# A two-layer transformer kernel on one core: host-side feature-major inputs, NSA scores from split queries and keys, and a later start of the modulation stream

## The chip, the core and the metric

The kernel runs on one core of one Trainium2 chip. The metric is the device time of one execution in microseconds (us). Engines are named as the profile names them: PE is TensorE's matrix multiplication, PEld its weight load, DVE is VectorE, ACT is ScalarE, POOL is GpSimd, SP is SyncE.

## The reference, cut to what matters

There are S = 256 tokens of D = 2048 features, all in float32. The first block is an NSA attention mixer followed by a gated feed-forward layer; the second has its norms, shifts and gates modulated by a vector `c`, and holds an attention layer and an MLP.

```python
h    = rmsnorm(x) * mix_norm_g
proj = h @ nsa_w_in               # queries (16 heads of 128), three keys/values, gates
# per head: the scores q.k for the compressed keys (15), the selected and the window
# branch; softmax of each, gated, and o = sum over branches of p @ v
x = x + concat(o) @ nsa_w_out
x = x + ffn(rmsnorm(x))           # ffn_w_in, ffn_w_out: the largest weights of block 1

mod = silu(c) @ w_mod + b_mod     # c has 2048 entries, w_mod is 2048 x 12288
sh1, sc1, g1, sh2, sc2, g2 = split(mod, 6)
h = rmsnorm(x) * (1 + sc1) + sh1
x = x + g1 * attention(h)         # w_in, w_uq, w_ukv, w_out
h = rmsnorm(x) * (1 + sc2) + sh2
x = x + g2 * (relu(h @ w_ff1) ** 2 @ w_ff2)
out = rmsnorm(x) * final_norm_g
```

## The kernel before, in words

Every large product is made from three reduced-precision products. A float32 operand is split by `split` (L84 on ACT writes the high part, L85 on DVE the rest), and `mm3` issues three matmuls, high by high, high by low and low by high, from L127, L128 and L129. The residual `h` and the normalised inputs `x` lie feature-major: features on the 128 partitions, the 256 tokens along the row.

`gemm` streams the weights. One tile holds 2 x 128 features by 512 columns (1 MB at most): a DMA of SP's queue fills `raw` (5 buffers), ACT makes `whi` and DVE makes `wlo` (4 buffers each, 128x1024), and PE runs 24 matmuls of 256 columns with them. After every tile `step()` advances two generators: `inner`, small work of the current layer, and `fill`, a background stream. `fill` is advanced `rate` steps for each 64th of a unit of work.

The background stream is `modulation`. For each of ten segments of 1024 columns (two more run in the last MLP) `mod_columns` loads 16 tiles `mw` of 128x1024 (L736, POOL's queue, two buffers; 192 loads in all), and DVE adds each times a column of `csil` into `macc` (L740, L742). `after(ld)` ties each load to the last matmul that had been issued, so that the loads follow PE's progress. At a segment's end eight small matmuls (L723) sum `macc` over the partitions, four copies (L726) gather the sums and L727 stores them to `modv`. The stream begins before the gemm of the fourth group of keys, inside `nsa()`, with rate 4.2, and runs through the NSA scores and the feed-forward layer.

At the start `norm_x` loads `x` token-major into eight tiles `xt`, transposes them on PE (32 transposes, L341), and from the banks ACT and DVE make the split, scaled `x` (L345, L346) while DVE copies `h` (L348). ACT squares `xt` with an accumulated sum (L354); the rows' `rstd` comes from these sums. The first gemm of `nsa_w_in` uses the `x` pairs one after another, as they come.

Vectors (`mix_norm_g`, `vec1`, `pos`, the pieces of `b_mod`) are loaded as rows and turned into columns by a transpose on PE (L228).

In `nsa_head` the scores of a head are float32 matmuls of `qT` with `kT`: one of 271 columns (L588), one of 15 (L589), two of 256 (L608). A float32 matmul shows as two passes in the trace (x2 beside the row).

The order of the instructions on each engine is not written by hand. The framework's scheduler decides it from its own model of times, so that a change in one place can move rows elsewhere. `nsa()`, `norm_x()` and the rest are called by `run` at L1015 and following.

Of the kernel before, what the change touches and what calls it, by code (L numbers as in the profile page):

```python
# [66 lines left out]
class Kernel:  # L67
# [209 lines left out]
    def vectors(self):  # L277
        nc, a, m = self.nc, self.a, self.main
        vec1 = self.columns([(self.vec("ffn_norm_g", 16), 16), (self.vec("final_norm_g", 16), 16),
                             (self.vec("attn_norm_g_2", 16), 16), (self.vec("mlp_norm_g_2", 16), 16),  # L280
                             (self.vec("mla_q_norm_g_2", 3), 3), (self.vec("mla_kv_norm_g_2", 1), 1),
                             (self.vec("c_2", 16), 16)], "vec1")
# [41 lines left out]
    def norm_x(self):  # L324

        nc, a = self.nc, self.a
        self.gmix = self.columns([(self.vec("mix_norm_g", 16), 16)], "gmix", nc.sync)
        xs = [self.pair("x") for _ in range(KT)]
        xt = []
        for s in range(8):  # L330
            xt.append(self.main.tile([128, 2, S], F32, name="xt", tag="u", bufs=16))
# [3 lines left out]
        banks = (("O", 1), ("PT", 1), ("S", 2), ("S", 2))  # L335
        for s in range(8):
            p = self.bank(*banks[s % 4])
            k = 2 * s
            for i in range(2):
                for t in range(2):  # L340
                    nc.tensor.transpose(p[:, i * S + t * 128:i * S + (t + 1) * 128],  # L341
                                        xt[s][:, t, i * 128:(i + 1) * 128], self.ident)
            for i in range(2):
                g, pi = self.gmix[:, k + i:k + i + 1], p[:, i * S:(i + 1) * S]
                nc.scalar.activation(xs[k + i][:, 0, :], pi, AF.Copy, scale=g)  # L345
                nc.vector.scalar_tensor_tensor(xs[k + i][:, 1, :], pi, g, xs[k + i][:, 0, :].bitcast(F32),  # L346
                                               op0=OP.mult, op1=OP.subtract)
            nc.vector.tensor_copy(self.h[:, k:k + 2, :].rearrange("p k n -> p (k n)"), p)  # L348
        ssq = self.main.tile([128, 2, 8], F32, name="ssq")

        def squares():
            for s in range(8):
                for t in range(2):
                    nc.scalar.activation(self.slast[:, t * S:(t + 1) * S], xt[s][:, t, :], AF.Square,  # L354
                                         accum_out=ssq[:, t, s:s + 1])
                yield
        self.inner = squares()
        return xs, ssq

    def rstd_x(self, ssq):  # L360
        for _ in self.inner:
            pass
        rc = self.main.tile([128, 2], F32, name="rc_x")
        self.nc.vector.tensor_reduce(rc, ssq, AX.X, OP.add)
        self.nc.vector.tensor_scalar(rc, rc, 1.0 / D, EPS, op0=OP.mult, op1=OP.add)
        return self.rsqrt(rc, self.main, "rcx")
# [29 lines left out]
    def nsa(self, xs, ssq, mp):  # L396
        nc, a, tc = self.nc, self.a, self.tc
        W, LD = a["nsa_w_in"], 5168
        with ExitStack() as es:
# [4 lines left out]
            kT = p.tile([128, 4, 528], F32, name="kT")  # L404
# [7 lines left out]
            with tc.tile_pool(name="cmp", bufs=1) as cp:  # L412
                dtab = self.bias_table("rel_bias", 0, cp)
                pos = self.columns([(a["cmp_pos_k"].rearrange("a b c -> (a b) c"), 32),
                                    (a["cmp_pos_v"].rearrange("a b c -> (a b) c"), 32)], "pos")
# [19 lines left out]
                def evk(br):  # L435
                    def f(i, b):
                        for j in range(2):
                            kg = kT[:, 2 * i + j, :].rearrange("p (t n) -> p t n", n=264)
                            kg = bass.AP(tensor=kg.tensor, offset=kg.offset + 128 * br,
                                         ap=[list(kg.ap[0]), [272, 2], [1, 128]])  # L440
                            nc.vector.tensor_tensor(kg, b[:, j * S:(j + 1) * S].rearrange("p (t n) -> p t n", n=128),
                                                    r1.rearrange("p (t n) -> p t n", n=128), OP.mult)
# [9 lines left out]
                self.fill, self.rate = self.modulation(mp, range(10)), 4.2  # L452
# [30 lines left out]
            for g in range(4):  # L483
# [4 lines left out]
                def evq(i, b):  # L488
                    qT[i] = w.tile([128, 2, S], F32, name="qT", tag="qT", bufs=2)
                    nc.vector.tensor_tensor(qT[i], b.rearrange("p (a n) -> p a n", n=S),  # L490
                                            rq[:, None, :].to_broadcast([128, 2, S]), OP.mult)
                self.gemm(W, LD, 0, xs, [(512 * g, 512)], evq)
                for j in range(4):
                    os_.append(self.nsa_head(w, 4 * g + j, g, qT[j // 2][:, j % 2, :], bt[:, j, :],
# [28 lines left out]
    def compress(self, cp, ku, kT, vcc):  # L523
# [35 lines left out]
        nc.vector.tensor_copy(kT[:, :, 256:271], po[:, :60].rearrange("p (g c) -> p g c", c=NCMP))  # L559
# [19 lines left out]
    def nsa_head(self, w, hd, g, q, bt, kT, vt, vcc, gate):  # L579
# [4 lines left out]
        pt = w.tile([128, 10, 128], F32, name="pt", tag="pt", bufs=2)  # L584
# [607 lines left out]
```

## Time and profile before

| | us |
|---|---|
| median of the runs (3) | 2123.52 (2122.17 to 2125.51) |
| profiled execution, its own time | 2119.85 |
| its span | 2118.0 |
| PE busy | 2094.1 (99%) |
| DVE busy | 1452.0 (69%) |
| ACT busy | 1017.1 (48%) |

The span runs from the first instruction to the last in the profile of one execution; that execution's own time is 1.85 us longer, and the median lies 3.67 us above that time. Busy is the time in which an engine had at least one instruction under way. The core's granted TensorE clock was at its full level in every fortieth of the span but for the first microseconds. The stretches are the start (0 to 36 us: loads, first gemm), NSA (to about 340 us), its output product and the feed-forward layer (to about 1110 us), the second block's attention and the MLP.

### The profile page before, as it was taken

The numbers are of one execution on the slowest core, as the hardware profiler recorded it, in microseconds if no ns is written. First come the engines' busy times: TensorE is split into PE (matmuls) and PEld (weight loads), VectorE is DVE, ScalarE is ACT, GpSimd is POOL, SyncE is SP. The second block draws the span as 40 slices with busy tenths as digits, with TensorE's granted clock in tenths as the row PEclk, the third lists the DMA queues.
The fourth block names the chain that finished last, engine by engine and source line by source line (L and its number), as shares of the span: only waits on it lengthen the run. The fifth ranks groups of instructions, "written<-read, shape, count | busy, mean of one in ns | idle before, by whom it ended". The sixth has DMA issues, their size and how long they took to land. (4 is left out here: it accounts for less than half of the span.)

```text
span 2118.0 us, 40943 instructions
## 1 busy us (share of the span) xinstructions
PE 2094.1 (99%) x16405; PEld 1992.5 (94%) x16405; DVE 1452.0 (69%) x2144; ACT 1017.1 (48%) x1504; POOL 162.9 (8%) x297
## 2 busy tenths in 40 slices
PE   9999999999999999999999999999999999999998
PEld 8899999999999999999999999899889989989987
DVE  7467876787777777877867676677676555555556
ACT  6334655554434434443445465565434534534543
POOL 2211000010110111101000000000100000000000
PEclk9999999999999999999999999999999999999999
DMA  8778555889889888888975663568887656656663
GB/s 277 261 234 311 170 163 180 286 265 296 276 282 303 274 301 281 279 294 276 298 233 156 182 183 112 160 196 280 283 294 233 194 191 194 193 193 193 192 194 133
DMA packets 288302, 492.29 MB, mean 232 GB/s; under 512 B 27111, under 2 KB 139338, under 8 KB 287856
## 3 DMA queue, kind: packets, MB, share of 16 engines
q1 hardware_dynamic: 254128, 371.20, 55.2%
q0 software_dynamic: 33408, 117.70, 16.7%
q8 instruction: 128, 2.10, 0.4%
q10 hardware_dynamic: 576, 0.79, 0.1%
q14 instruction: 62, 0.51, 0.1%
HBM read 487.21 MB, written 2.20 MB: 231 GB/s over the span
## 5 line engine op out<-in xcount | busy, mean ns | idle before, releaser
L84 ACT ACTIVATE whi<-raw 128x1024 fp32r<-128x1024 f32 (+2 forms) x716 | 746.2, 1044 | 904.8 <-PE acc L128 645.4
L85 DVE TENSOR_TENSOR wlo<-raw,whi 128x1024 fp32r<-128x1024 f32 (+2 forms) x716 | 853.5, 1200 | 392.1 <-ACT whi L84 378.8
L127 PE MATMUL acc<-x,whi 128*128 128x256 f32 x3184 | 882.6, 278 | 3.2 <-ACT v L463 1.4
L128 PE MATMUL acc<-x,whi 128*128 128x256 f32 x3184 | 884.3, 278 | 0.0
L129 PE MATMUL acc<-x,wlo 128*128 128x256 f32 x3184 | 882.7, 278 | 0.2 <-DVE wlo L85 0.2
L127 PEld LDWEIGHTS acc<-x,whi 128*128 128x128 f32 x3184 | 597.8, 188 | 8.6 <-issue 5.0
L128 PEld LDWEIGHTS acc<-x,whi 128*128 128x128 f32 x3184 | 599.4, 188 | 5.4 <-issue 4.6
L129 PEld LDWEIGHTS acc<-x,wlo 128*128 128x128 f32 x3184 | 599.0, 188 | 1.4 <-DVE wlo L85 0.6
L742 DVE SCALAR_TENSOR_TENSOR macc<-mw,csil,macc 128x1024 f32<-128x1024 f32 x180 | 231.1, 1284 | 175.0 <-DMA mw<-w_mod 174.1
L128 PE MATMUL acc<-u,whi 128*128 128x256 f32 x1260 | 349.7, 279 | 0.8 <-DVE u L85 0.8
L127 PE MATMUL acc<-u,whi 128*128 128x256 f32 x1260 | 346.3, 280 | 1.0 <-DVE h L642 0.6
L129 PE MATMUL acc<-u,wlo 128*128 128x256 f32 x1260 | 347.0, 278 | 0.0
L128 PEld LDWEIGHTS acc<-u,whi 128*128 128x128 f32 x1260 | 236.7, 188 | 1.9 <-DVE u L85 1.5
L127 PEld LDWEIGHTS acc<-u,whi 128*128 128x128 f32 x1260 | 234.9, 188 | 3.2 <-ACT u L84 1.0
L129 PEld LDWEIGHTS acc<-u,wlo 128*128 128x128 f32 x1260 | 235.9, 188 | 0.7 <-issue 0.2
L164 PE MATMUL acc<-whi,u 128*128 128x512 f32 (+1 forms) x544 | 206.2, 379 | 0.0
L165 PE MATMUL acc<-wlo,u 128*128 128x512 f32 (+1 forms) x544 | 206.1, 379 | 0.0
L163 PE MATMUL acc<-whi,u 128*128 128x512 f32 (+1 forms) x544 | 204.4, 376 | 0.0
L736 POOL DMA_DIRECT2D mw<-w_mod x192 | 102.6, 534 | 1003.2 <-PE acc L129 657.7
L164 PEld LDWEIGHTS acc<-whi,u 128*128 128x128 f32 x544 | 102.2, 188 | 20.6 <-issue 0.4
L163 PEld LDWEIGHTS acc<-whi,u 128*128 128x128 f32 x544 | 102.1, 188 | 20.3
L165 PEld LDWEIGHTS acc<-wlo,u 128*128 128x128 f32 x544 | 102.2, 188 | 18.4
(349 smaller groups left out, 1316.9 us busy)
## 6 DMA issues: line engine op xcount, KB each, us to landing
raw<-w_ff SPq DMA_DIRECT2D x256, 512.0 KB, 4.1
mw<-w_mod POOLq DMA_DIRECT2D x192, 512.0 KB, 5.6
raw<-ffn_w_in SPq DMA_DIRECT2D x352, 256.0 KB, 5.0
raw<-ffn_w_out SPq DMA_DIRECT2D x87, 512.0 KB, 5.3
raw<-nsa_w_in SPq DMA_DIRECT2D x72, 512.0 KB, 5.3
raw<-nsa_w_out SPq DMA_DIRECT2D x32, 512.0 KB, 4.5
raw<-w_out SPq DMA_DIRECT2D x32, 512.0 KB, 4.0
raw<-w_in SPq DMA_DIRECT2D x24, 512.0 KB, 3.9
```

The source lines that it names most:

```text
L84: self.nc.scalar.activation(hi, x, AF.Copy)
L85: self.nc.vector.tensor_tensor(lo, x, hi.bitcast(F32), OP.subtract)
L127: mm(out, wh, xh, start=first, stop=False, skip_group_check=True)
L128: mm(out, wh, xl, start=False, stop=False, skip_group_check=True)
L129: self.last = mm(out, wl, xh, start=False, stop=last, skip_group_check=True)
L163: mm(o, xt[:, 0, q], hi, start=k == 0, stop=False)
L164: mm(o, xt[:, 1, q], hi, start=False, stop=False)
L165: self.last = mm(o, xt[:, 0, q], lo, start=False, stop=k == nk - 1)
L736: ld = nc.gpsimd.dma_start(wt, self.src(self.a["w_mod_2"], k * 128 * LD + s * 1024, [[LD, 128], [1, 1024]]))
L742: nc.vector.scalar_tensor_tensor(acc, wt, csil[:, k:k + 1], acc, op0=OP.mult, op1=OP.add)
```

## The change

The host now also passes `x` transposed (`l_xT`) and the small vectors as columns (`l_gmix`, `l_vec1`, `l_pos`, `l_bmod`). The kernel loads `x` straight into `h`; the 32 transposes, the copies and four of the five kinds of vector transpose go. The sum of squares is made as in the other norms: `square_sums` squares pairs of feature tiles (ACT), DVE adds them into `sacc`, and `rstd_col` sums over the partitions by one-column matmuls (L244 of the kernel before). Queries and keys of NSA are split once after they are made, and the scores are `mm3` products. `modulation` starts after `nsa()`, with rate 5.05 in place of 4.2.

```diff
@@ def vectors(self):
-        vec1 = self.columns([(self.vec("ffn_norm_g", 16), 16), (self.vec("final_norm_g", 16), 16),
...
+        vec1 = m.tile([128, 84], F32, name="vec1")
+        nc.gpsimd.dma_start(vec1, a["l_vec1"])
@@ def norm_x(self):
-        self.gmix = self.columns([(self.vec("mix_norm_g", 16), 16)], "gmix", nc.sync)
+        self.gmix = self.main.tile([128, 16], F32, name="gmix")
+        nc.sync.dma_start(self.gmix, a["l_gmix"])
...
-            nc.sync.dma_start(xt[s], self.src(a["x"], s * S, [[D, 128], [128 * D, 2], [1, S]]))
+            nc.sync.dma_start(self.h[:, 2 * s:2 * s + 2, :],
+                              self.src(a["l_xT"], 256 * s * S, [[S, 128], [128 * S, 2], [1, S]]))
...
-                    nc.tensor.transpose(p[:, i * S + t * 128:i * S + (t + 1) * 128],
-                                        xt[s][:, t, i * 128:(i + 1) * 128], self.ident)
...
-                nc.scalar.activation(xs[k + i][:, 0, :], pi, AF.Copy, scale=g)
...
-            nc.vector.tensor_copy(self.h[:, k:k + 2, :].rearrange("p k n -> p (k n)"), p)
-        ssq = self.main.tile([128, 2, 8], F32, name="ssq")
+        for k in range(KT):
+            g, x = self.gmix[:, k:k + 1], self.h[:, k, :]
+            nc.scalar.activation(xs[k][:, 0, :], x, AF.Copy, scale=g)
+            nc.vector.scalar_tensor_tensor(xs[k][:, 1, :], x, g, xs[k][:, 0, :].bitcast(F32),
+                                           op0=OP.mult, op1=OP.subtract)
+        sums = self.square_sums()
         def squares():
...
+            for k in range(0, KT, 2):
+                sums(k)
                 yield
...
-    def rstd_x(self, ssq):
+    def rstd_x(self, _):
...
+        return self.rstd_col(self.sums(self.cD[:, 0:1]), EPS, self.main, "rcx")
@@ def nsa(self, xs, ssq):
-            kT = p.tile([128, 4, 528], F32, name="kT")
+            kT = p.tile([128, 2, 4, 528], F32R, name="kT")
...
+                            self.split(t[:, j, :].rearrange("p (t n) -> p t n", n=128), kg[0], kg[1])
...
-                self.fill, self.rate = self.modulation(mp, range(10)), 4.2
                 self.gemm(W, LD, 0, xs, [(4096, 512)], evk(1))
...
-                    qT[i] = w.tile([128, 2, S], F32, name="qT", tag="qT", bufs=2)
+                    qf = w.tile([128, 2, S], F32, name="qf", tag="qf", bufs=1)
+                    qT[i] = w.tile([128, 2, 2, S], F32R, name="qT", tag="qT", bufs=2)
...
+                    self.split(qf, qT[i][:, 0], qT[i][:, 1])
@@ def nsa_head(...):
+        def score(out, q, c, n=1):
+            k = [kT[:, l, g, c].rearrange("p (b n) -> p b n", b=n) if n > 1 else kT[:, l, g, c] for l in range(2)]
+            self.mm3(out, q[:, 0], q[:, 1], k[0], k[1], True, True)
...
-        mm(s[:, 0:271], q0, kT[:, g, 0:271], start=True, stop=True)
-        mm(s[:, 272:287], q1, kT[:, g, 256:271], start=True, stop=True)
+        score(s[:, 0:272], q0, slice(0, 272))
+        score(s[:, 272:288], q1, slice(256, 272))
@@ def run(self):
+        os_ = self.nsa(xs, ssq)
         mp = self.ctx.enter_context(tc.tile_pool(name="mod", bufs=1))
-        os_ = self.nsa(xs, ssq, mp)
+        self.fill, self.rate = self.modulation(mp, range(10)), 5.05
@@ def mod_cols(self, o, n, name):
-        bv = self.columns([(self.vec("b_mod_2", n, 128 * o), n)], "b_")
+        bv = self.main.tile([128, n], F32, name="bv", tag="colb", bufs=1)
+        self.nc.gpsimd.dma_start(bv, self.a["l_bmod"][:, o:o + n])
+def layouts(a):
+    def cols(*names):
+        return np.ascontiguousarray(np.concatenate([a.pop(n).reshape(-1, 128).T for n in names], 1))
+    return {"l_xT": np.ascontiguousarray(a.pop("x").reshape(S, D).T), "l_gmix": cols("mix_norm_g"),
...
```

The scheduler's order moves at three places. The first is ACT at the very start, where it makes the first `x` pairs and splits the first weight tiles. Before:

```order
L345 ACTIVATE x<-PT,gmix 128x256
L84 ACTIVATE whi<-raw 128x1024
L354 ACTIVATE slast,ssq<-xt 128x256 x3
L345 ACTIVATE x<-PT,gmix 128x256
L354 ACTIVATE slast,ssq<-xt 128x256
L84 ACTIVATE whi<-raw 128x1024
```

These are the second and the third weight tile, with the squares of the old form between them. The same place on ACT after the change, where L335 makes the high part of `x`, L642 squares, and L294 and L287 are functions of `vectors`:

```order
L84 ACTIVATE whi<-raw 128x1024
L335 ACTIVATE x<-h,gmix 128x256 x4
L642 ACTIVATE slast<-h 128x512
L294 ACT_TABLE_LOAD
L294 ACTIVATE csil<-vec_748 128x16
L84 ACTIVATE whi<-raw 128x1024
L335 ACTIVATE x<-h,gmix 128x256 x4
L642 ACTIVATE slast<-h 128x512
L287 ACT_TABLE_LOAD
L287 ACTIVATE both<-botht 128x16
L84 ACTIVATE whi<-raw 128x1024
```

Four conversions of `x`, a square and a table load now stand between one weight tile and the next, twice. The second place is PE at a head of NSA; before, the last scores of one head and the first of the next read so (`S` is a bank of scores, `acc` that of the next gemm):

```order
L608 MATMUL S_2268<-kT_224,qT_2238 128x2x128 x2
L127 MATMUL acc_2465<-x_99,whi_2562 128x256
L588 MATMUL S_2298<-kT_224,qT_2238 128x271
L589 MATMUL S_2298<-kT_224,qT_2238 128x15
L128 MATMUL acc_2465<-x_99,whi_2562 128x256
```

After the change the scores of one head are twelve rows:

```order
L127 MATMUL S_2197<-kT_160,qT_2124 128x272
L128 MATMUL S_2197<-kT_160,qT_2124 128x272
L129 MATMUL S_2197<-kT_160,qT_2124 128x272
L127 MATMUL S_2197<-kT_160,qT_2124 128x16
L128 MATMUL S_2197<-kT_160,qT_2124 128x16
L129 MATMUL S_2197<-kT_160,qT_2124 128x16
L127 MATMUL S_2226<-kT_160,qT_2124 128x2x128
L128 MATMUL S_2226<-kT_160,qT_2124 128x2x128
L129 MATMUL S_2226<-kT_160,qT_2124 128x2x128
L127 MATMUL S_2226<-kT_160,qT_2124 128x2x128
L128 MATMUL S_2226<-kT_160,qT_2124 128x2x128
L129 MATMUL S_2226<-kT_160,qT_2124 128x2x128
```

Each float32 matmul became three with the split parts of `kT` and `qT`. The third place is DVE in the feed-forward layer, where `macc` is made between the `wlo` of the weight stream. Before, in the middle of the stream:

```order
L85 TENSOR_TENSOR wlo_6651<-raw_6647,whi_6650 128x1024
L740 TENSOR_SCALAR macc_6513<-mw_6514,csil_833 128x1024
L85 TENSOR_TENSOR wlo_6695<-raw_6692,whi_6694 128x1024
L85 TENSOR_TENSOR wlo_6728<-raw_6725,whi_6727 128x1024
L742 SCALAR_TENSOR_TENSOR macc_6513<-mw_6579,csil_833,macc_6513 128x1024
L85 TENSOR_TENSOR wlo_6758<-raw_6755,whi_6757 128x1024
```

After the change, a stretch of the same kind (L731 is what was L742):

```order
L731 SCALAR_TENSOR_TENSOR macc_5863<-mw_6531,csil_760,macc_5863 128x1024
L85 TENSOR_TENSOR wlo_6715<-raw_6712,whi_6714 128x1024
L85 TENSOR_TENSOR wlo_6755<-raw_6752,whi_6754 128x1024
L731 SCALAR_TENSOR_TENSOR macc_5863<-mw_6596,csil_760,macc_5863 128x1024
L85 TENSOR_TENSOR wlo_6785<-raw_6782,whi_6784 128x1024
```

Where two `wlo` stood between every pair of `macc` rows, one and two now alternate.

## Rows read from the trace of the kernel before

**Rows 1.** Page, part 1: busy time, share of span, instructions per engine

```profile
PE 2094.1 (99%) x16405; PEld 1992.5 (94%) x16405; DVE 1452.0 (69%) x2144; ACT 1017.1 (48%) x1504; POOL 162.9 (8%) x297
```

**Rows 2.** PE's longest wait, whole span: total us, times, longest

```profile
PE PT L341 <- DMA xt<-x: 3.0, 1, 3.0
```

**Rows 3.** Windows, feed-forward: us, busy PE PEld DVE ACT POOL, PEclk, DMA share, GB/s

```profile
375.00:1110.00 735.00, 733.20 (x6475) 728.21 (x6474) 565.64 (x604) 324.37 (x363) 74.52 (x141) 1.00 0.86 282
550.00:600.00 50.00, 50.00 (x444) 50.00 (x443) 38.12 (x37) 21.25 (x22) 5.28 (x10) 1.00 0.87 289
```

**Rows 4.** Windows at the start, same columns

```profile
5.00:10.00 5.00, 2.02 (x12) 1.78 (x11) 2.79 (x5) 3.78 (x12) 2.48 (x6) 0.80 1.04 308
...
15.00:20.00 5.00, 5.00 (x46) 5.00 (x45) 4.06 (x7) 5.00 (x19) 0.00 (x0) 1.00 1.07 374
```

**Rows 5.** Timeline of PE at the start: start us, us, instruction, [idle before, releaser]

```profile
8.41 1.12 PE L341 MATMUL PT<-ident,xt 128*128 128x128 f32 x4 [2.98 <-DMA xt<-x]
9.18 0.56 PE L127 MATMUL acc<-x,whi 128*128 128x256 f32 x1
```

**Rows 6.** Timeline of ACT at the start

```profile
11.03 1.06 ACT L84 ACTIVATE whi<-raw 128x1024 fp32r<-128x1024 f32 x1 [0.98 <-DMA raw<-nsa_w_in]
...
17.16 0.82 ACT L345 ACTIVATE x<-S,gmix 128x256 fp32r<-128x256 f32 x2
...
21.13 1.07 ACT L84 ACTIVATE whi<-raw 128x1024 fp32r<-128x1024 f32 x1
...
23.89 1.28 ACT L261 ACT_TABLE_LOAD   x1
```

**Rows 7.** Groups of instructions: busy us, mean ns, idle before: a 512-column square

```profile
L653 ACT ACTIVATE slast<-h 128x512 f32<-128x512 f32 (+1 forms) x22 | 13.3, 604 | 9.9 <-DVE sacc L659 5.8 <-DVE h L642 4.1
```

**Rows 8.** Timeline of PE behind the first gemm

```profile
36.09 0.28 PE L128 MATMUL acc<-x,whi 128*128 128x256 f32 x1
36.29 0.27 PE L228 MATMUL S<-ident,vrows 64*128 64x64 f32 x1
...
36.72 0.28 PE L127 MATMUL acc<-x,whi 128*128 128x256 f32 x1
```

**Rows 9.** Timeline of PE at one head of NSA

```profile
232.25 0.62 PE L588 MATMUL S<-kT,qT 128*128 128x271 f32 x2
232.71 0.29 PE L589 MATMUL S<-kT,qT 128*128 128x15 f32 x2
232.85 1.11 PE L608 MATMUL S<-kT,qT 128*128 128x256 f32 x4
233.61 0.47 PE L128 MATMUL acc<-x,whi 128*128 128x256 f32 x1
233.91 0.28 PE L129 MATMUL acc<-x,wlo 128*128 128x256 f32 x1
```

**Rows 10.** Timeline of PE at the feed-forward norm's column of sums

```profile
440.12 0.50 PE L244 MATMUL S<-cD,sacc 128*128 128x1 f32 x4
440.48 1.03 PE L244 MATMUL S<-cD,slast 128*128 128x1 f32 x8
...
441.57 0.28 PE L127 MATMUL acc<-x,whi 128*128 128x256 f32 x1
...
446.28 0.28 PE L128 MATMUL acc<-x,whi 128*128 128x256 f32 x1
```

**Rows 11.** Tile mw, 100 to 355 us, then whole span: ns min/median/max, starts; landings

```profile
L736 POOL DMA_DIRECT2D mw<-w_mod x32: 527/528/564, 108.5 to 346.6; - x32
...
L742 DVE SCALAR_TENSOR_TENSOR macc<-mw,csil,macc x180: 1276/1285/1291, 118.5 to 1595.4; 128x1024 f32<-128x1024 f32 x180
...
DMA to landing us min/median/max: 3.8/5.6/8.3
```

**Rows 12.** Timeline of POOL: one load of mw

```profile
505.85 0.53 POOL L736 DMA_DIRECT2D mw<-w_mod  x1 [4.91 <-PE acc L129]
```

**Rows 13.** DVE's longest wait from 450 to 1050 us

```profile
DVE macc L742 <- DMA mw<-w_mod: 89.1, 69, 3.1
```

More of the change, by code (lines that the diff above doesn't have):

```diff
@@ L349, in norm_x @@
-        ssq = self.main.tile([128, 2, 8], F32, name="ssq")
+        for k in range(KT):
[4 more added lines that the diff above has]
+        sums = self.square_sums()
         def squares():
[L352 to L355, printed above, removed]
+            for k in range(0, KT, 2):
+                sums(k)
@@ L356, in squares @@
                 yield
         self.inner = squares()
-        return xs, ssq
-    def rstd_x(self, ssq):
+        return xs, None
+    def rstd_x(self, _):
         for _ in self.inner:
             pass
[L363 to L366, printed above, removed]
+        return self.rstd_col(self.sums(self.cD[:, 0:1]), EPS, self.main, "rcx")
@@ L413, in nsa @@
                 dtab = self.bias_table("rel_bias", 0, cp)
-                pos = self.columns([(a["cmp_pos_k"].rearrange("a b c -> (a b) c"), 32),
-                                    (a["cmp_pos_v"].rearrange("a b c -> (a b) c"), 32)], "pos")
+                pos = cp.tile([128, 64], F32, name="pos")
+                nc.gpsimd.dma_start(pos, a["l_pos"])
                 ku = cp.tile([128, 2, 32, 60], F32, name="ku")
@@ L436, in f @@
                     def f(i, b):
+                        t = cp.tile([128, 2, S], F32, name="kf", tag="kf", bufs=2)
+                        nc.vector.tensor_tensor(t, b.rearrange("p (a n) -> p a n", n=S), r2, OP.mult)
                         for j in range(2):
[L438 to L442, printed above, removed]
+                            kg = [kT[:, l, 2 * i + j, :] for l in range(2)]
+                            kg = [bass.AP(tensor=g.tensor, offset=g.offset + 128 * br,
+                                          ap=[list(g.ap[0]), [272, 2], [1, 128]]) for g in kg]
+                            self.split(t[:, j, :].rearrange("p (t n) -> p t n", n=128), kg[0], kg[1])
                     return f
@@ L558, in compress @@
             nc.tensor.matmul(po[:, :60], w2[0][:, mt, :], ht[:, mt, :], start=mt == 0, stop=mt == 1)
-        nc.vector.tensor_copy(kT[:, :, 256:271], po[:, :60].rearrange("p (g c) -> p g c", c=NCMP))
+        self.split(po[:, :60].rearrange("p (g c) -> p g c", c=NCMP), kT[:, 0, :, 256:271], kT[:, 1, :, 256:271])
         po = self.bank("S", 2)
@@ L582, in nsa_head @@
         self.wp = w
-        pt = w.tile([128, 10, 128], F32, name="pt", tag="pt", bufs=2)
-        q0, q1 = q[:, 0:128], q[:, 128:256]
+        pt = w.tile([128, 8, 128], F32, name="pt", tag="pt", bufs=2)
+        q0, q1 = q[:, :, 0:128], q[:, :, 128:256]
+        def score(out, q, c, n=1):
+            k = [kT[:, l, g, c].rearrange("p (b n) -> p b n", b=n) if n > 1 else kT[:, l, g, c] for l in range(2)]
+            self.mm3(out, q[:, 0], q[:, 1], k[0], k[1], True, True)
         s = self.bank("S", 2)
-        mm(s[:, 0:271], q0, kT[:, g, 0:271], start=True, stop=True)
-        mm(s[:, 272:287], q1, kT[:, g, 256:271], start=True, stop=True)
+        score(s[:, 0:272], q0, slice(0, 272))
+        score(s[:, 272:288], q1, slice(256, 272))
         sb = self.sb0[hd % 2]
@@ L603, in nsa_head @@
             nc.tensor.transpose(pp[:, i * 128:(i + 1) * 128], sb[:, i * 128:(i + 1) * 128], self.ident)
-        nc.scalar.activation(pt[:, 0:10:3, :], pp.rearrange("p (a b) -> p a b", b=128), AF.Copy)
+        nc.scalar.activation(pt[:, 0:4, :], pp.rearrange("p (a b) -> p a b", b=128), AF.Copy)
         s = self.bank("S", 2)
         for t in range(2):
-            mm(s.rearrange("p (b t n) -> p t b n", t=2, n=128)[:, t], q1,
-               kT[:, g, 272 * t:272 * t + 256].rearrange("p (b n) -> p b n", n=128), start=True, stop=True)
+            score(s.rearrange("p (b t n) -> p t b n", t=2, n=128)[:, t], q1, slice(272 * t, 272 * t + 256), 2)
         sb = w.tile([128, 512], F32, name="sb1", tag="sb1", bufs=2)
@@ L1185 @@
     arrays.update(constants())
+    arrays.update(layouts(arrays))
     aps = {n: nc.dram_tensor(n, v.shape, mybir.dt.from_np(v.dtype), kind="ExternalInput").ap()
```

35 lines of the change are left out of this document (12 added, 23 removed).

## The prediction

> **What bounds the kernel now.** I read the page's busy shares first: PE is busy 99% of the span, and the next engine, DVE, 69% [rows 1]. Then the waits of PE: the longest single one is 3.0 us, at the start, for a tile of `x` [rows 2]. So PE's own instructions bound the kernel nearly everywhere; an instruction that leaves or joins PE's stream counts in full behind the start, and other engines' work counts only where PE would wait for it. Two stretches have to be read apart. In the feed-forward layer PE is busy 733.20 of 735 us, the DMA engines are busy 0.86 of the time and move 282 GB/s; a quiet 50 us there hold 444 matmuls of 256 columns, so one costs 50/444 = 0.1126 us [rows 3]. At the start PE is busy only 2.02 of 5 us between 5 and 10 us, at a granted clock of 0.80, while ACT is busy the whole of 15 to 20 us and the DMA engines move 374 GB/s [rows 4]. The start is therefore bound by arriving bytes first and by ACT next, and the rest by PE.
>
> **The sum's base.** The profiled execution took 2119.85 us (span 2118.0), the median of the runs is 3.67 us above it. I make the sum against 2119.85 and add 3.67 at the end. A change of 0.2%, 4.2 us, is about what a measurement of this kernel can tell from none.
>
> **Scores.** A head's scores run from 232.25 to the gemm matmul behind them, which ends 233.91 and takes 0.11: 233.91 - 0.11 - 232.25 = 1.55 us [rows 9], for two passes of 271 columns, four of 256 and two of 15 (a float32 matmul shows as two). The first pair starts 0.46 before the next row, 0.23 each; at the same price per column the four of 256 cost 0.215 each; what is left, 1.55 - 0.46 - 0.86 = 0.23, is 0.117 for each narrow pass. After the change there are three matmuls of 272 columns, three of 16 and six of 256. At the split matmuls' price, 0.1126 us for 256 columns, 272 cost 0.120; the narrow ones I take at the 0.117 just read. 0.36 + 0.35 + 0.68 = 1.39 us a head, 0.16 less, rounded down to 0.15 for 16 heads: **-2.4 us**. Bounds: if a narrow pass cost nothing after, 0.50 less a head, -8; if it cost 0.14 (the time between the starts of L589 and L608, as if one pass filled it) and the wide ones the 0.118 per 256 columns that is read below, 1.51, -0.6.
>
> The narrow price is the term to doubt. The twelve one-column passes of the norm take from 440.12 to 441.57, less one gemm matmul of 0.11, so 1.34/12 = 0.111 us each [rows 10]; a matmul of one column costs as much as one of 256. [...]
>
> The split itself adds a step between a group's query gemm and its first score: an ACT copy and a DVE subtraction of 512 columns, some 0.5 and 0.7 us (a 512-column ACT pass is 0.604 [rows 7]). In the order, 24 to 35 other matmuls, 2.7 to 3.9 us, stand between, against about 60 before, and DVE has no `macc` (1.285 us [rows 11]) in its queue there any more. I take 0; the bound is 1 us in each of four groups, +4.
>
> **The start.** Removed are the 32 transposes and DVE's eight copies into `h`. The first gemm matmul now starts at 9.18, behind a wait of 2.98 us for the second `xt` and its transposes, and the gemm ends at 36.09 - 0.11 = 35.98 [rows 5, 8]. Its 192 matmuls alone take 192 x 0.1126 = 21.6, so 26.8 - 21.6 = 5.2 us in it are transposes, low clock and waits. With `x` directly in `h`, one tile of it is enough, and the first matmul can start near 7.6. But the weight tiles set the pace behind it. The second `whi` starts at 11.03 when its bytes land [rows 6] and ends at 12.1 as before. ACT then does, by its new order, four parts of `x` (0.41 each, half of 0.82), a square (0.604), a table load (1.28) and a small function before the next `whi` (1.07) [rows 6, 7]: 1.64 + 0.5 + 1.28 + 0.2 + 1.07, about 4.7. So `whi` number 3 ends at 16.8, number 4, behind the second table load, at 21.4, number 5, behind four parts and a square, at 24.7, with `wlo` 1.2 later at 25.9 (before, the fifth tile's `whi` began at 21.13 [rows 6]). From there four tiles of 24 matmuls remain, 10.8 us: the gemm ends near 36.4, **+0.4 us**. [...]
>
> **The norm's column and the vectors.** `rstd_col` adds twelve passes of 0.111 to PE, **+1.3 us** [rows 10]. Vector transposes on PE: in [rows 8] L228 lies between 36.09 and 36.72, in which two more gemm matmuls have 0.23, so it costs 0.40; three of these go behind the start, **-1.2 us**. Their DMAs of columns (one for each) come over POOL, and nobody waits for them at once; I take 0.
>
> **A slower pace after one-column passes.** From 441.57 to 446.28, behind the norm's column, 40 matmuls take 4.71 us, 0.1178 each [rows 10], against 0.1126 in the quiet stretch [rows 3]. In the trace this pace ends at the next column sum of the modulation (L723). In the order that is some 57 matmuls behind the norm before, and some 420 after, because the stream starts later. 363 x 0.0045 = **+1.6 us**, bounds 0 and +2.
>
> **The modulation stream.** Of the 160 loads of the ten segments, 32 lay in NSA [rows 11]; now all lie behind it. 32 x 0.524 MB is 16.8 MB over 735 us, 23 GB/s beside 282: 305 GB/s, a DMA share of 0.93. The start shows that 374 GB/s can be moved [rows 4], so the weights still arrive. The pair of `mw` buffers is nearer to its limit. A load now comes every 0.53 + 4.91 = 5.44 us, the time of 48 matmuls [rows 12]; after, 48 and 24 alternate, so two loads come in 72 matmuls, 8.1 us. A buffer's cycle is issue 0.53, landing 5.6 (median; 3.8 to 8.3) and `macc` 1.285, 7.4 us [rows 11]: it fits, with 0.7 us to spare. DVE has already waited 89.1 us for `mw` in 69 `macc`, up to 3.1 us at a time [rows 13], and behind a waiting `macc` stand the `wlo` of PE's next tiles. DVE's busy time grows by 32 x 1.285 = 41 us in 735, from 0.77 to 0.83. A part of the landings will be late; I take 0.3 us for each of ten segments, **+3 us**, bounds 0 and +15. [...]
>
> NSA gives back the `macc` that ran there, which is off PE's path: 0. Block 2 and the MLP keep their order: 0.
>
> **The sum**: -2.4 + 0.4 + 1.3 - 1.2 + 1.6 + 3 = +2.7 us, 2122.55 for a profiled execution, and 2122.55 + 3.67 = **2126** as a median.
>
> **Rivals.**
> 1. *The stream becomes the bound of the feed-forward layer* (slower). At a landing of 6.3 us a buffer's cycle reaches the 8.1 us of two loads. At 6.5 each pair is 0.2 late, 1.6 by the end of a segment's eight pairs, so that L723 and PE wait there ten times: +10 to +16 beside the sum's +3, a median of about 2134 to 2140. For it speak the 89.1 us of waits; against it the 374 GB/s of the start.
> [...]
> 3. *The start gains in full* (faster): if ACT's table loads and squares fall into times when the next raw tile hasn't landed anyway, -6.8 in place of +0.4 leaves the sum at -4.5, a median of 2119, and 2116 if the stream costs nothing as well. For it: the second tile lands only at 11.03. Against it: ACT is busy all of 15 to 20 us.
> [...]
>
> **How the numbers follow.** The forecast's sum has 0.50, with a range of its own from 2121 to 2130; of that 0.42 lies within 0.2% and 0.08 above. Rival 1 has 0.17, rival 2 0.10, rival 3 0.18, rival 4 0.05. Faster is rival 3, 0.18; the same is 0.42 + 0.05 = 0.47; slower is 0.08 + 0.17 + 0.10 = 0.35. The range runs from 2117 (most of rival 3) to 2136 (rival 2 and the lower part of rival 1) and leaves out about 0.2.
>
> **What would show it.** In the profile after: the first gemm matmul near 7.6 and the second gemm's first near 36.5; a score block of 1.39 us at a head; twelve L244 passes of 1.3 us behind the start; 40 matmuls at 0.118 until the first L723 of the feed-forward layer; a DMA share near 0.93 there and landings of `mw` near 6 us, with PE's waits at L723 under 0.5 us each. The prediction is wrong if the first gemm ends below 33, if PE in the feed-forward layer loses more than 8 us to waits, or if a head's scores take 1.2 us or less.

## The result, and the profile after

The changed kernel takes 2205.86 us (median of four runs, 2205.63 to 2208.45), the kernel before 2124.52 in the same comparison: a ratio of 1.0389 (95% interval 1.0376 to 1.0402), 81 us slower. The forecast was 2126, no change, with a range to 2136. The profiled execution has a span of 2206.7 us against 2118.0.

The page's first part reads as before [rows 1], with PE busy for 99%:

```profile
span 2206.7 us, 41053 instructions
...
PE 2178.3 (99%) x16445; PEld 2071.0 (94%) x16445; DVE 1464.2 (66%) x2150; ACT 1019.5 (46%) x1496; POOL 159.3 (7%) x291
```

PE has 40 instructions more and 84.2 us more busy time, of 88.7 us between the two spans, and DVE and ACT hardly any: so PE isn't waiting for a new bound, its own instructions take longer. The windows of the feed-forward layer [rows 3] show the same; the columns are us, then busy us and instructions of PE, PEld, DVE, ACT and POOL, the granted clock, the DMA share and GB/s:

```profile
375.00:1110.00 735.00, 730.83 (x6102) 724.78 (x6102) 573.49 (x602) 303.70 (x338) 85.95 (x161) 1.00 0.89 289
```

In the same 735 us PE issues 6102 matmuls in place of 6475, at the same granted clock of 1.00 and with 2.4 us more idle. 730.83/6102 is 119.8 ns for one, 733.20/6475 was 113.2. PE's waits have grown little; the longest of the stretch is below, and the wait at the column sums, for which the prediction looked, is 0.8 us in all (us in total, times, longest):

```profile
PE acc L127 <- DVE h L631: 1.8, 1, 1.8
PE acc L129 <- DVE wlo L85: 1.3, 2, 1.0
PE S L712 <- DVE macc L731: 0.8, 1, 0.8
```

So nearly all of the loss came from no wait, no transfer and no added instruction. By the start times in the trace a product matmul of 256 columns costs 120.0 ns from start to start, all through the program. In the kernel before it cost 113.3 for most of the time and 117.8 for the rest, 113.9 in the mean. With 13,332 of them (3 x 3184 and 3 x 1260 in the profile's groups), 6.1 ns are 81 us. The 1440 of 512 columns, which take the weights as their moving operand, go from 229 to 234 ns, 7 us more; the work that the change removed gives some of it back.

What differs for these matmuls is where their tiles lie. The framework allocates the tiles of a pool one behind the other, and the change took small tiles out of it. No view of the profile shows addresses; the table's differences follow from the sizes of the tiles in the order in which the two programs ask for them. The bytes at which the tiles of the two built programs start on each partition, and the distance of the weights from the moving operand modulo 256:

```
kernel     x      u       raw     whi     wlo      whi-x   whi-u   (mod 256)
before   39200   71968  104736  125536  141920       64      64
after    38176  124288   70944   91424  107808        0     160
```

Before, two small tiles stood ahead of `whi`: the sums `ssq` (64 bytes) and `pos` (256). All the other tiles between `x` and `whi` are whole multiples of 2 KB, so these 320 bytes alone made the distance 64. The change needs no `ssq`, and puts `pos` in another pool: 0. And `u`, whose buffers `xt` had claimed ahead of `raw`, now comes behind the weights and three 32-byte places of `rstd_col`: 160.

### The profile page after: what moved, and what is told of

Read it like the earlier page. It is cut to its first block, busy times and chain, and to the rows that moved or that the text cites. A ratio compares the mean times of both kernels' runs of the same rounds, so it can differ in the third digit from the quotient of the medians.

```text
span 2206.7 us, 41053 instructions
## 1 busy us (share of the span) xinstructions
PE 2178.3 (99%) x16445; PEld 2071.0 (94%) x16445; DVE 1464.2 (66%) x2150; ACT 1019.5 (46%) x1496; POOL 159.3 (7%) x291
## 5 line engine op out<-in xcount | busy, mean ns | idle before, releaser
L127 PE MATMUL acc<-x,whi 128*128 128x256 f32 x3184 | 903.4, 285 | 5.6 <-ACT whi L84 4.4
L129 PE MATMUL acc<-x,wlo 128*128 128x256 f32 x3184 | 902.0, 284 | 2.2 <-DVE wlo L85 2.1
L128 PE MATMUL acc<-x,whi 128*128 128x256 f32 x3184 | 903.7, 284 | 0.3 <-DVE x L923 0.2
L127 PEld LDWEIGHTS acc<-x,whi 128*128 128x128 f32 x3184 | 611.5, 192 | 12.6 <-ACT whi L84 6.3
L128 PEld LDWEIGHTS acc<-x,whi 128*128 128x128 f32 x3184 | 612.6, 192 | 4.9 <-issue 3.7
L129 PEld LDWEIGHTS acc<-x,wlo 128*128 128x128 f32 x3184 | 611.8, 192 | 3.8 <-DVE wlo L85 3.5
L128 PE MATMUL acc<-u,whi 128*128 128x256 f32 x1260 | 355.4, 283 | 0.8 <-DVE u L85 0.8
L129 PE MATMUL acc<-u,wlo 128*128 128x256 f32 x1260 | 353.8, 283 | 1.0 <-DVE wlo L85 1.0
L127 PE MATMUL acc<-u,whi 128*128 128x256 f32 x1260 | 351.7, 284 | 2.2 <-DVE h L631 1.8
L731 DVE SCALAR_TENSOR_TENSOR macc<-mw,csil,macc 128x1024 f32<-128x1024 f32 x180 | 231.0, 1283 | 136.9 <-DMA mw<-w_mod 136.1
L164 PE MATMUL acc<-whi,u 128*128 128x512 f32 (+1 forms) x544 | 208.2, 383 | 0.0
L163 PE MATMUL acc<-whi,u 128*128 128x512 f32 (+1 forms) x544 | 208.2, 383 | 0.0
```

Of the source, the lines that this page charges most:

```text
L127: mm(out, wh, xh, start=first, stop=False, skip_group_check=True)
L128: mm(out, wh, xl, start=False, stop=False, skip_group_check=True)
L129: self.last = mm(out, wl, xh, start=False, stop=last, skip_group_check=True)
L163: mm(o, xt[:, 0, q], hi, start=k == 0, stop=False)
L164: mm(o, xt[:, 1, q], hi, start=False, stop=False)
L731: nc.vector.scalar_tensor_tensor(acc, wt, csil[:, k:k + 1], acc, op0=OP.mult, op1=OP.add)
```

## The experiments

**Moving the weights by 64 bytes, or everything.** The first run sets 64 unused bytes between `x` and the weights, the second the same bytes ahead of `x`:

```diff
+        pad = self.main.tile([128, 16], F32, name="pad")      # second run: here
+        nc.gpsimd.memset(pad, 0.0)
         xs = [self.pair("x") for _ in range(KT)]
+        pad = self.main.tile([128, 16], F32, name="pad")      # first run: here
+        nc.gpsimd.memset(pad, 0.0)
```

> The changed kernel with 64 unused bytes on each partition placed behind the x pairs, so that raw, whi, wlo and u all lie 64 bytes higher and x stays. Nothing else changes. Theory A (the place of the weight tiles against x sets what a split matmul costs: in the kernel before whi and x differ by 64 modulo 128 bytes, in the changed one by 0): the pace goes back from 120 ns per 256-column matmul to about 113, and the time to 2115 to 2130 us. Theory B (a state of TensorE that the removed transposes or float32 scores used to leave): pace 120, time 2200 to 2210 as for the changed kernel. Theory C (the modulation stream, all in the feed-forward layer, slows the matmuls there): no difference from the changed kernel either, 2200 to 2210.

> The changed kernel with the same 64 unused bytes placed ahead of the x pairs, so that x, raw, whi, wlo and u all move by 64 bytes together. Theory A in its relative form (only the difference of x and weights counts): pace 120 ns, 2200 to 2210 us. Theory A in its absolute form (the weights' own place modulo 128 counts, which is 96 here as in the kernel before): pace 113, 2115 to 2130 us. Theories B and C: 2200 to 2210 us.

The first took 2159.86 us (ratio 1.0181, 1.0166 to 1.0197), the second 2204.73 (1.0395, 1.0380 to 1.0411). 64 bytes that no instruction uses for its work gave back 46 us, and the same bytes ahead of `x` gave back nothing. Neither theory B nor C allows the first, and the absolute form of A doesn't allow the second: it is the distance between the operands. In the first run the gemms that read `x` are at 64 again, those that read `u` still at 160, so half comes back, where the expectation of 2115 to 2130 had not reckoned with `u`: by its trace a matmul on `x` costs 114.9 ns in the mean and one on `u` 119.9, and 5.1 ns for the 9552 on `x` are 49 us.

**The kernel before with 64 bytes.** The reverse: nothing of the change, only `whi` and `wlo` 64 bytes higher.

```diff
         ssq = self.main.tile([128, 2, 8], F32, name="ssq")
+        pad = self.main.tile([128, 16], F32, name="pad")
+        nc.gpsimd.memset(pad, 0.0)
```

> The kernel before with 64 unused bytes placed ahead of whi, so that whi and wlo lie 64 bytes higher while x, u and raw stay. Work and order stay. Theory A: x and whi now differ by 0 modulo 128 bytes as in the changed kernel, the pace falls to 120 ns and the time rises to 2190 to 2215 us. Theories B and C: no change, 2120 to 2127 us.

It took 2190.74 us (1.0327, 1.0309 to 1.0344), 69 us slower with the same work in nearly the same order. The expectation named 0 modulo 128 as the bad place; modulo 256, the distance is 128. Its windows from 600 to 1000 us, under those of the second run, with the same columns:

```profile
600.00:1000.00 400.00, 400.00 (x3346) 397.15 (x3345) 307.89 (x313) 160.15 (x171) 46.24 (x87) 1.00 0.89 289
```

```profile
600.00:1000.00 400.00, 400.00 (x3380) 397.72 (x3379) 294.61 (x298) 161.16 (x172) 38.86 (x73) 1.00 0.84 275
```

400 us over 3346 and 3380 is 119.5 and 118.3 ns: two prices, neither the 113 of before, with PE never idle.

**A map of the price.** To see the price without the DMA, ACT and DVE traffic of the kernel, a small kernel runs nothing but `mm3` blocks and shifts the weights against `x`:

```diff
+    for d in range(0, 2048, 32):
+        for t in range(8):      # eight one-column passes
+            mm(acc[:, 128 * t:128 * t + 1], xr[:, t * 128:t * 128 + 128], col, start=True, stop=True, ...)
+        gemm(d, 4)              # 96 matmuls with the weights d bytes further on
+        for j in range(4):      # four matmuls of a ones column
+            mm(acc[32 * j:32 * j + 1, S * j:S * j + S], ones, xr[:, S * j:S * j + S], ...)
+        gemm(d, 4)
```

> A kernel that leaves out the whole computation and measures the disputed cost by itself: split-product matmuls (stationary 128 x 128, moving 128 x 256, high and low parts of x 1024 bytes apart, as mm3 issues them) in blocks of 96, for 64 distances of the weights from x, 0 to 2016 bytes modulo 2048 in steps of 32; each distance once behind eight one-column passes and once behind four matmuls of a ones column, the two kinds behind which the kernel before was seen to leave one pace for the other. Theory A: the pace depends on the distance: near 120 ns at 0 and at 1952 (the changed kernel's x and u), 113 or 118 at 320 (before), 118 to 120 at 384 (the padded kernel before), 113 or 120 at 64; other distances unknown. Rival: no dependence on the distance without the DMA, ACT and DVE traffic of the full kernel, all blocks near 113.

Mean ns from one start to the next, by the trace's start times, for each distance modulo 256. The first matmuls of each block are left out. The eight repetitions up to 2048 bytes agree within 0.1:

```
distance              0     32     64     96    128    160    192    224
behind one-column   119.9  118.4  117.8  117.4  118.7  119.9  117.8  116.7
behind ones column  119.9  118.4  117.7  118.7  118.6  119.9  113.3  116.6
```

Four rows of its timeline show two of these blocks (start us, us, instruction): the first pair, at 160, is 81 matmuls apart, 9.71 us, 119.9 ns each; the second, at 192, 87 matmuls in 9.86 us, 113.3 each.

```profile
154.71 0.28 PE L55 MATMUL acc<-x,w 128*128 128x256 f32 x1
...
164.42 0.28 PE L55 MATMUL acc<-x,w 128*128 128x256 f32 x1
...
180.05 0.28 PE L55 MATMUL acc<-x,w 128*128 128x256 f32 x1
...
189.91 0.28 PE L55 MATMUL acc<-x,w 128*128 128x256 f32 x1
```

The rival falls: with no other traffic the price still hangs on the distance. 0 and 160, the changed kernel's two distances, are the two worst of eight, 119.9; its 120.0 is accounted for. 128 gives 118.7, which the trace of the padded kernel before shows. 64 is not single-valued: the map has 117.8 there, and the kernel before keeps 113.3 in long stretches and 117.8 in others. In this map only 192 shows both values, and 96 two others.

**The whole change at the distance of before.** `u` is allocated behind `x`, and 320 unused bytes stand ahead of `whi`:

```diff
         xs = [self.pair("x") for _ in range(KT)]
+        u = self.pair("u")
+        nc.gpsimd.memset(u[:, 0, 0:8].bitcast(F32), 0.0)
...
+        gap = self.main.tile([128, 80], F32, name="gap")
+        nc.gpsimd.memset(gap[:, 0:8], 0.0)
         sums = self.square_sums()
```

> The changed kernel with everything it does, but with the tiles placed so that the distances are those of the kernel before: u is allocated behind x, and 320 unused bytes ahead of whi, so that whi and wlo lie 320 bytes above x and u modulo 2048 (64 unused bytes alone left u at another distance and gave back only half). Theory A (distance of weights from the moving operand modulo some power of two): pace 113 to 118 ns everywhere, 2122 to 2135 us, which is the kernel before plus what the late modulation costs (10 us) less the scores' 2 or 3. Rival (something else of the change holds the slow pace as well, in the gemms that read u or in the feed-forward layer): above 2150 us.

2130.25 us (1.0027, 1.0015 to 1.0040). Of the 3.89% all but 0.27% is gone, with every part of the change in it. Its window from 600 to 1000 us, where the second run above had 3346 instructions:

```profile
600.00:1000.00 400.00, 400.00 (x3538) 397.18 (x3538) 323.27 (x330) 167.87 (x179) 48.98 (x92) 1.00 0.93 307
```

**The other distance.** If the map holds, 192 should do as well as 64: the kernel before with 128 unused bytes ahead of `whi`, and the changed one with 448 in place of 320.

```diff
+        pad = self.main.tile([128, 32], F32, name="pad")     # the kernel before
...
-        gap = self.main.tile([128, 80], F32, name="gap")     # the changed one
+        gap = self.main.tile([128, 112], F32, name="gap")
```

> The kernel before with 128 unused bytes ahead of whi: the weights now lie 448 bytes above x and u, 192 modulo 256 in place of 64. Work and order stay. Theory (the map: the pace depends on the distance modulo 256 bytes, and at 192 it is 113.3 ns behind one kind of entry and 117.8 behind another): a mixture of these two paces as in the kernel before, 2112 to 2135 us. If the kernel before has its mixture for another reason than its distance of 64: anything else, 120 ns and 2200 us among it. If only equal places modulo 128 hurt (192 and 64 are the same there): as before within 5 us.

> The changed kernel with u behind x and 448 unused bytes ahead of whi (192 modulo 256 for x and u). By the map a mixture of 113.3 and 117.8 ns; 2115 to 2135 us, with 2130 if the mixture is that of the run at 64 and 2113 if nearly all matmuls keep 113.3.

2172.65 us (1.0223, 1.0196 to 1.0250) and 2164.32 (1.0190, 1.0163 to 1.0217), above both expectations. The paces are the two of the map, but not in the proportion that I took: by the start times in the traces 97% and 77% of the product matmuls run at the slower one, against 13% in the kernel before and 27% in the changed one at 64.

```profile
600.00:1000.00 400.00, 400.00 (x3405) 397.71 (x3404) 298.33 (x303) 163.08 (x174) 39.53 (x74) 1.00 0.86 278
```

This is the kernel before at 192: 400/3405 is 117.5 ns. A distance can thus have two paces. Which of them holds changes nearly always where something interrupts the stream of product matmuls, and then stays: in the trace of the kernel before, 30 of the 32 unbroken stretches of 37 or more product matmuls keep one pace throughout, the longest for 791.

**High and low weights at distances of their own.** The map again, over pairs, with a third kind of entry:

> A kernel that leaves out the whole computation: the blocks of the first map (48 matmuls each) with the distance of the high weights and of the low weights from x set apart, each 0 to 224 bytes modulo 256, and three kinds of entry ahead of a block: eight one-column passes, four matmuls of a ones column, four float32 matmuls of 256 columns. Theory: where both distances are equal the paces of the first map come back (119.9 at 0, 118.4, 117.8, 117.4 to 118.7, 118.7, 119.9, 117.8 or 113.3 at 192, 116.7 at 224); apart, each third of the matmuls has the price of its own distance and the mean lies between. If a pair exists that keeps 113.3 behind all three entries, a placing would be better than that of the kernel before. Rival: the price is not one of the single distance, and some mixed pair lies outside both.

Equal pairs gave the first map's values, with exceptions that matter: 64 gave 113.3 behind two entries behind which the first map has 117.8, and 192 gave 117.8 behind all three. So the kind of entry doesn't by itself decide between the two paces. Most mixed pairs lie between 117.5 and 120, some outside their two single prices (122.1 for 64 and 96 behind one entry). One, 64 for the high part and 192 for the low, gave 113.9, 113.7 and 113.7 behind the three entries (113.3 once the block has run for ten matmuls), where 64 for both gave 113.3, 113.3 and 117.8. Put into the changed kernel by 128 unused bytes between `whi` and `wlo`:

> The changed kernel with the places of the run at 64, and 128 more unused bytes between whi and wlo: the high weights lie 64 bytes above x and u modulo 256, the low weights 192. By the second map this pair keeps 113.7 ns behind all three kinds of entry, where equal distances of 64 give 113.3 or 117.8. So nearly no matmul at 117.8, a mean of some 113.8 in place of the 114.6 of the run at 64, 12 us less than it: 2115 to 2122 us, a little below the kernel before. Rival (the map's small kernel leaves out what decides in the full one): 117.8 in long stretches as before, 2126 to 2135 us, or more.

2124.71 us (1.0016, 1.0006 to 1.0026), above the expected 2115 to 2122. The pace did what was expected: 5% of the product matmuls at the slower price. By the medians 5.5 us of the 12 were gained; by the two ratios, each against its own runs of the kernel before, it is 2 us, and their intervals overlap. In the profiled executions about 6 us went into longer waits of PE at the head of the feed-forward layer and a lower clock behind them, which come next. No version beat the kernel before.

**The parts, one by one.** At the distance of 64 the prediction's other terms can be priced: the late modulation alone in the kernel before; the host layout alone; and everything but the split scores.

```diff
-                self.fill, self.rate = self.modulation(mp, range(10)), 4.2       # late modulation
...
+        self.fill, self.rate = self.modulation(mp, range(10)), 5.05              # behind nsa()
```

> The kernel before with one part of the change alone: modulation started behind nsa() with rate 5.05. The places of x, whi and wlo don't change. Theory A: pace 113 ns, and only the stream's own cost is added, 2122 to 2132 us (the prediction's terms: 1.6 for the slower pace until the first column sum, 3 for late landings). Theory C: the feed-forward layer slows, 2150 us or more. Theory B: 2120 to 2132 us.

> The kernel before with the host layout alone (x, gmix, vec1, pos and b_mod feature-major; float32 scores and the modulation's early start with rate 4.2 stay), and with the same placing as the run beside it, 320 bytes between x or u and the weights modulo 2048. The prediction's terms for this part are 0.4 for the start, 1.3 for the norm's column and -1.2 for the vector transposes, together 0.5 us: 2118 to 2126 us beside the kernel before. If the start gains in full: 5 to 7 us less than the kernel before. Without theory A (places don't matter and the layout itself is what slows the matmuls): about 2200.

> The changed kernel with the places of the run at 64 modulo 256, but with the float32 scores of the kernel before (host layout and late modulation stay). Against that run it prices the split scores: by the prediction they save 2.4 us (0.15 a head), so 2130 to 2135 us here, 2.4 above that run; if the bound of free narrow passes holds, 8 above it; if the split costs waits, below it.

Late modulation: 2132.47 us (1.0052, 1.0037 to 1.0067), 11 us. Layout: 2128.70 (1.0023, 1.0012 to 1.0034), 5 us. Everything but the scores: 2137.09 (1.0072, 1.0047 to 1.0097), so the scores are worth 6.8 us by the medians and 9.5 by the ratios, with wide intervals. All three lie above their expected ranges, by 0.5 to 2.7 us. In the last one's profiled execution, the longest of six, 33% of the matmuls were at the slower pace against 27%, which would be some 3 us of it (0.06 x 13,332 x 4.5 ns).

Where the late modulation costs shows in two windows. First the kernel before, then the same with the late modulation alone, then the changed one with 64 and 192, whose pace is nearly that of the kernel before:

```profile
360.00:480.00 120.00, 118.59 (x1042) 117.62 (x1042) 97.13 (x115) 60.81 (x76) 11.86 (x23) 1.00 0.85 276
500.00:1080.00 580.00, 579.61 (x5125) 575.59 (x5125) 443.64 (x457) 246.92 (x266) 59.01 (x110) 1.00 0.87 286
```

```profile
360.00:480.00 120.00, 112.80 (x953) 111.75 (x952) 98.32 (x114) 55.10 (x70) 14.87 (x28) 0.96 0.86 281
500.00:1080.00 580.00, 577.89 (x5086) 573.60 (x5086) 464.06 (x477) 243.70 (x263) 70.88 (x133) 1.00 0.92 304
```

```profile
360.00:480.00 120.00, 112.27 (x962) 111.04 (x961) 98.88 (x116) 56.50 (x72) 14.90 (x28) 0.98 0.88 288
500.00:1080.00 580.00, 580.00 (x5129) 576.06 (x5128) 469.48 (x480) 245.41 (x264) 70.79 (x133) 1.00 0.93 307
```

From 500 to 1080 us little is lost to waits: 1.7 us more with the late modulation alone (the rest of its 39 missing matmuls is the slower pace) and nothing in the last kernel, although the DMA share is 0.93 and 307 GB/s move. Between 360 and 480 PE is idle 5.8 and 6.3 us more, but it issues 89 and 80 matmuls fewer, which are 10 and 9 us of its work. The rest is the clock, 0.96 and 0.98 in these rows against 1.00. With the late modulation alone the longest wait there is 3.5 us, and behind it the granted clock is 0.50 (first the wait, as above; then a window with the columns as above):

```profile
PE acc L127 <- DVE h L641: 3.5, 1, 3.5
```

```profile
377.00:381.00 4.00, 4.00 (x21) 4.00 (x21) 4.00 (x8) 3.97 (x10) 0.53 (x1) 0.50 0.93 355
```

The matmuls there start 0.213 us apart. Behind this wait and the next, of 2.8 us, 39 matmuls do so, which costs 3.9 us beside 6.3 us of waits. With 64 and 192, where three waits are about 2 us, the row reads 0.96 from 360 to 400 us and 0.97 from 440 to 480, where the kernel before has 1.00. The timeline of DVE in that kernel (start us, us, instruction, [idle before, releaser]), and three waits of PE in the same window:

```profile
444.54 1.28 DVE L738 SCALAR_TENSOR_TENSOR macc<-mw,csil,macc 128x1024 f32<-128x1024 f32 x1 [1.88 <-DMA mw<-w_mod]
445.74 1.22 DVE L85 TENSOR_TENSOR wlo<-raw,whi 128x1024 fp32r<-128x1024 f32 x1
446.88 0.16 DVE L265 RECIPROCAL rf<-rf 128x2 f32<-128x2 f32 x1
...
473.05 1.28 DVE L738 SCALAR_TENSOR_TENSOR macc<-mw,csil,macc 128x1024 f32<-128x1024 f32 x1 [3.45 <-DMA mw<-w_mod]
```

```profile
370.55 0.36 PE L130 MATMUL acc<-u,whi 128*128 128x256 f32 x1 [1.85 <-DVE h L638]
...
448.79 0.71 PE L276 MATMUL S<-ident,rf 128*128 128x128 f32 x4 [2.28 <-DVE rf L268]
...
476.72 0.39 PE L132 MATMUL acc<-x,wlo 128*128 128x256 f32 x1 [2.04 <-DVE wlo L85]
```

At 444 us DVE stands at a `macc` whose `mw` is late; behind it stand the small steps of the norm's `rf`, and PE waits for them. At 473 us it is a `wlo` that comes behind such a `macc`.

## Why the prediction was wrong

**The step that failed** is the base of the sum. It took every instruction that the change doesn't touch at its duration of before ("one costs 50/444 = 0.1126 us", "Block 2 and the MLP keep their order: 0"), and asked only what is added, removed or waited for. The change moved the operands of all 13,332 product matmuls of 256 columns to another distance, which raised their price from 113.9 to 120.0 ns in the mean. That is 81 us, and 7 more with the matmuls of 512 columns, beside which the terms of the sum are small. No rival held it, and the order of the instructions couldn't show it; the allocation of the built program did. It was shown both ways: the kernel before slows by 69 us with 64 unused bytes, and the changed one loses all but 0.27% of its 3.89% with 320 and another place for `u`. None of the three signs of being wrong that the prediction named for itself came: behind the first gemm the column passes start at 39.5 us, PE loses 4.2 us to waits in the feed-forward layer, and a head's scores take 1.42. All three look at waits and at added work, none at the price of an instruction that the change leaves alone.

A sign of it stood in the rows. The 0.1178 us after the one-column passes [rows 10] was read as their after-effect, +1.6 us (with the 0.1126 that it names beside it, 363 matmuls would be 1.9). It is the second of the two paces of the distance 64; the one-column passes are one of several places where it changes. With 64 and 192 it is nearly absent though the passes stay.

**Scores**, -2.4, near right: the block of a head, forecast at 1.39 us, runs from 245.79 to 247.21 in the changed kernel, 1.42 against 1.55 [rows 9], 0.13 x 16 = 2.1 us:

```profile
245.79 0.29 PE L127 MATMUL S<-kT,qT 128*128 128x272 f32 x1
...
246.17 0.17 PE L127 MATMUL S<-kT,qT 128*128 128x16 f32 x1
246.19 0.26 PE L128 MATMUL S<-kT,qT 128*128 128x16 f32 x1
246.31 0.26 PE L129 MATMUL S<-kT,qT 128*128 128x16 f32 x1
246.42 0.36 PE L127 MATMUL S<-kT,qT 128*128 128x256 f32 x1
246.62 0.29 PE L128 MATMUL S<-kT,qT 128*128 128x256 f32 x1
...
247.21 0.28 PE L127 MATMUL acc<-x,whi 128*128 128x256 f32 x1
```

The three narrow passes and the wide one behind them take 0.45, from 246.17 to 246.62; less 0.12 for a wide one, that is 0.11 for each narrow one, near the 0.117 taken. The start that follows another by 0.02 is no price of its own: the wide pass behind the three has 0.20 until the next start. The 0.05 that the chances give a rival 4 stands for narrow passes far below the 0.117, an estimate that no run shows: they cost 0.11 us with 16 columns here, and 0.111 with one [rows 10]. No wait for the split of `q` appears among PE's waits: that bound was not needed.

**Start**, +0.4: right in its mechanism. In the whole change at the distance of 64 the first gemm matmul starts at 8.31 (forecast 7.6), behind a wait for the first `whi`, and the first one-column pass behind the gemm at 36.77, where 36.4 was forecast; the working's own 25.9 + 10.8 gives 36.7.

```profile
8.31 0.58 PE L127 MATMUL acc<-x,whi 128*128 128x256 f32 x1 [1.97 <-ACT whi L84]
...
36.77 0.50 PE L244 MATMUL S<-cD,sacc 128*128 128x1 f32 x4
```

PE's waits for `whi` and `wlo` up to there, 4.9 us, use up what the first `x` gains. Rival 3, whose -6.8 is the 1.6 us between 9.18 and 7.6 and the 5.2 of the first gemm, falls. The 0.10 that the chances give a rival 2, and with it a part of the range up to 2136, stands for a start that loses the clock, +5 us, an estimate that no run shows: the matmuls start 0.21 us apart until 11.7 us, where the kernel before has this until 11.2, and 0.11 to 0.12 from there, but for waits; that is a few matmuls. (The granted clock reads 1.00 from 5 to 20 us in the profile of the changed kernel, also where its matmuls start 0.21 apart, until 12.1, so at the start this row is no witness.) **The norm's column**, +1.3, was twelve passes as forecast.

**The stream**, +3, was mis-sized and misplaced: alone it costs 11 us. Of the 12.6 us between the spans of the two profiled executions, 5.6 are idle time of PE, some 4 the lower clock behind the waits, which no term held, and some 3.5 a larger share of matmuls at the slower pace (19% against 13%). In the long stretch, where rival 1 put the danger, it costs 2 us or nothing in waits; the DMA share is 0.92 to 0.93, and `mw` lands in 5.9 to 6.0 us in the median, both near the forecast. It costs at its beginning, where DVE's queue holds small steps and `wlo` tiles behind a `macc`. In the changed kernel itself these waits are shorter (0.2 us at `rf`), perhaps because the slower PE leaves DVE more time; no run tests that.

**Layout** (the start, the norm's column and the vectors): 5 us where 0.5 was forecast. The profile taken of that run has 38% of its matmuls at the slower pace, and the profiled execution was its longest, so I can't say which part is the layout's work and which the pace.

What decides between the two paces of one distance stays open (not the kind of entry alone, as the second map shows), and why the price has a period of 256 bytes: the runs show that it has, and no more.

## What to carry to other kernels

When a change adds, drops or reorders tiles, compare the addresses of the matmuls' two operands in both built programs before anything is priced; 64 unused bytes ahead of the weights cost the kernel before 3.3% (2190.74 us). When a kernel with PE busy for 99% slows, divide busy time by matmuls in a stretch without waits: if the quotient moved, as it did here from 113.2 to 119.8 ns, look at the operands and not at the queues. The late background stream was dearest where the engine that it uses also carries a short serial chain: PE's idle time grew by 5.8 us between 360 and 480 us, with the granted clock at 0.96 there, and by 1.7 us from 500 to 1080. Starting it beside long uniform work and not at a norm would be worth a run, which was not made here.

## What the runs showed of the hardware that I had not expected

The price of a 256-column split matmul whose weights are reloaded each time (16445 weight loads for 16445 matmuls in the changed kernel) depends on the distance in SBUF between the weights and the moving operand: in the maps and kernels here 113.3 to 120.0 ns, 6%, at a granted clock of 1.00, and with a period of 256 bytes, as the map's eight repetitions up to 2048 bytes agree within 0.1 ns. It needs no other traffic, since it appears in a kernel that does nothing else (119.9 ns at 160, 113.3 at 192), and moving both operands together changes nothing (2204.73 us against 2205.86). Some distances have two paces, 113.3 and 117.8 ns at 64 and at 192, and the stream mostly keeps one of them until it is interrupted (30 of 32 long stretches in the kernel before). With the late modulation alone the granted clock was 0.50 behind a wait of 3.5 us in the middle of the program (377 to 381 us), and 39 matmuls behind this wait and one of 2.8 us cost 0.213 us in place of 0.113. No wait for another engine goes with the price: from 600 to 1000 us PE is busy 400.00 of 400 us in the kernel before with 64 bytes more, at 118.3 ns. No run shows why it hangs on where the two operands lie.
